# The order of each engine's list, made along a simulated time line instead of from a plain table of durations

## The chip, the cores and the metric

One core of one Trainium2 chip. The time is that of one execution on the device in microseconds, the median of several runs. Five engines have queues of their own, which run in order: TensorE (PE, with its weight loads as PEld), VectorE (DVE), ScalarE (ACT), GpSimd (POOL) and SyncE (SP), which issues the DMAs. They wait for each other by semaphores.

## The reference

Two transformer blocks over 512 rows of width 1024, in float32. The first has a mixer of two halves, 2-D neighbourhood attention with context keys and a Mamba-2 scan (SSD) in both directions, then a gated FFN with a convolution, then a norm. The second has windowed attention with a sink, then a SwiGLU FFN. Modulations come from products of a vector with ada_w.

```python
h = modulate(rms_norm(x, norm1_w), sh1, sc1)
p = h @ w_in
attn = neighbourhood_attention(q, k, v, kc, vc, rpb, rows)
y_ssd, _, _ = ssd_bidirectional(p[..., 3 * NA_WIDTH:col_ssd], xs, bm, cm, dt, a, ssd_d,
                                ssd_norm_w, h_fwd, h_bwd)
x = x + g1 * (jnp.concatenate([attn, y_ssd], axis=-1) @ w_out)
x = x + g2 * conv_glu(modulate(rms_norm(x, norm2_w), sh2, sc2), ffn_w_up, ffn_conv_w, ffn_conv_b, ffn_w_down)
x = rms_norm(x, final_norm_w)
...
x = x + g1 * rmsnorm(windowed_gqa_sink(h, att_w_qkv, att_w_o, att_sink, rel_bias), mix_norm_post)
x = x + g2 * rmsnorm(swiglu(h, ffn_w_in, ffn_w_out), ffn_norm_post)
```

## The kernel before

Every weight comes from memory in float32 as tiles of 128x1024 (`wr`, three buffers, DMA on SP in `fetch`, L132). `load_w` splits a tile in a high part (`wh`, ACT, L152) and a low part (`wl`, DVE, L153), and each product is three matmuls (`mm3`, L89 to L91; `step` in `nat_out`, L829). In between, `load_w` lets one step of the vector products with ada_w run (`gemv`: an `ada` tile by DMA, L226, and one operation on DVE, L230).

The stages in order, with the time at which they run: the prologue, where x and the rows of `ada` (L182) make the modulated features h for eight feature blocks of 128 (`gemv2`, L322; `columns`, L330; `features`, L342), to 70 us; the tiles of the projection, beginning with those for the scan (x_bc); the SSD (`ssd`, L590 to L640: L593 and L617 sums and products, L605 spreads, L629 and L634 outputs, on DVE and POOL between them) beside the first `project`s (rope on ACT, DVE, POOL, L681 to L684), about 112 to 197 us; neighbourhood attention (`attend`, L743 to L775) and the last projections, to 345; w_out and the first norm, to 397; the FFN; the norm into the second block at 755; the projections of the second attention from 777 and its heads from 811 to 919; w_o; the second FFN from 970.

A norm is turned to features by `turn` (L913, called by `tick` after a set count of products), and the features are split on DVE (L920, L921). In the second attention each head has four score tiles: PE L1053 and L1054 into a bank of scores (three of them), DVE L1056 adds the bias, ACT L1058 takes exp, PE L1069 transposes into one of two banks, ACT L1073 and DVE L1074 split, PE L1080 multiplies with v into one bank; ACT L1086 and DVE L1087 add its halves, and per pair of heads L1097 and L1098 divide. Products of the next projection (L89 to L91) are free to stand between these rows.

```python
        hi, lo = WH(F32R, 1024), WL(F32R, 1024)
        act(hi[:, :n], raw[:, :n], AF.Copy)
        V.tensor_sub(lo[:, :n], raw[:, :n], hi[:, :n])
        step_jobs()
...
                tr(pt[:, 128 * i:128 * i + 128], sc[:, 128 * i:128 * i + 128], ident)
...
            act(hi, src, AF.Copy)
            V.tensor_sub(lo, src, hi)
```

The order in which an engine gets its instructions is not that of the code. A scheduler takes every instruction as soon as what it needs is done by its reckoning, and writes one list for each engine. By default it reckons with a table of durations; nothing in the kernel sets an order by hand but the counts of `tick`.

## Time and profile before

| | |
|---|---|
| median of 3 runs | 1336.83 us (1335.62 to 1337.73) |
| the profiled execution | 1336.04 us, span 1334.2 |
| busy of the span | PE 97%, DVE 61%, ACT 45%, POOL 7% |
| DMA | 168.12 MB, mean 126 GB/s |

Busy time counts what an engine does; the rest of the span it waits. A PE that is 97% busy leaves little to be had. The windows cut the span by time: each row has a stretch, its length, and the busy time of PE, PEld, DVE, ACT and POOL in it with the number of instructions, then the clock granted to PE (1.00 is 2.4 GHz), the share of time in which the DMA engines were busy, and the rate. The chain of waits follows what ended last back to what released it.

### The profile page before, as it was taken

The page shows a single profiled execution, that of the slowest core. Times are in us where ns is not written, and L with a number is a line of the kernel's source. Part 1 is how long each engine was busy: PE and PEld are TensorE (multiplying, and loading weights), DVE is VectorE, ACT ScalarE, POOL GpSimd, SP SyncE. Part 2 cuts the span into 40 slices and gives each one's busy share as a digit, 9 for nine tenths or more (in the row PEclk, how much of TensorE's full clock was granted, in tenths as well). Part 3 has the DMA queues.
Part 4 walks back from the last instruction along what each step waited for, and adds up shares of the span by engine and source line. Part 5 has one row for each costly group of instructions (what it writes and reads, how often), then busy time and mean ns, then how long its engine had stood idle before and what let it go on. Part 6 is the DMA issues. An engine that isn't in the chain of part 4 may idle for free.

```text
span 1334.2 us, 17792 instructions
## 1 busy us (share of the span) xinstructions
PE 1296.5 (97%) x6751; PEld 1082.7 (81%) x6751; DVE 813.3 (61%) x1491; ACT 599.1 (45%) x1090; POOL 94.9 (7%) x101
## 2 busy tenths in 40 slices
PE   8999999999999999999999999999999999999997
PEld 4687778998879888888788788878798888888886
DVE  5887996566685766675953667997644232334333
ACT  3546546675454333333433557886652222233321
POOL 0013550000000000000000310000100000000000
PEclk9999999999999999999999999999999999999999
DMA  8763131133553654664754213112133333332221
GB/s 306 261 190 114 45 103 56 43 124 112 207 196 103 221 171 160 221 207 171 239 172 142 69 39 97 47 47 93 56 111 95 95 95 95 97 102 101 95 79 64
DMA packets 53237, 168.12 MB, mean 126 GB/s; under 512 B 6048, under 2 KB 11424, under 8 KB 53152
## 3 DMA queue, kind: packets, MB, share of 16 engines
q1 hardware_dynamic: 53152, 166.99, 38.5%
q8 instruction: 53, 0.87, 0.3%
q14 instruction: 32, 0.26, 0.1%
HBM read 164.87 MB, written 2.10 MB: 125 GB/s over the span
## 4 chain that ended last, share of the span: by engine, by line
PE 77%; DVE 10%; DMA 5%; ACT 4%; issue 2%; POOL 2%; SPq 0%; POOLq 0%; DVEq 0%; ACTq 0%
PE bank L829 18%; PE bank L90 16%; PE bank L89 16%; PE bank L91 16%; PE bank L769 2%; PE bank L1080 1%; DVE wl L153 1%; DMA ada<-in_ada_w 1%; PE bank L1069 1%; DMA wr<-in_w_in 1%; PE bank L763 1%; DVE acc L230 1%; POOL sm L211 1%; ACT wh L152 1%; DVE hl L921 1%
## 5 line engine op out<-in xcount | busy, mean ns | idle before, releaser
L90 PE MATMUL bank<-hl,wh 128*128 128x512 f32 (+1 forms) x1040 | 387.2, 372 | 2.1 <-DVE hl L921 1.5
L91 PE MATMUL bank<-hh,wl 128*128 128x512 f32 (+1 forms) x1040 | 387.7, 373 | 0.0
L89 PE MATMUL bank<-hh,wh 128*128 128x512 f32 (+1 forms) x1040 | 386.0, 373 | 0.1
L152 ACT ACTIVATE wh<-wr 128x1024 fp32r<-128x1024 f32 x173 | 182.2, 1058 | 386.3 <-PE bank L90 270.3
L153 DVE TENSOR_TENSOR wl<-wr,wh 128x1024 fp32r<-128x1024 f32 x173 | 212.9, 1232 | 196.6 <-ACT wh L152 196.2
L90 PEld LDWEIGHTS bank<-hl,wh 128*128 128x128 f32 x1040 | 196.4, 189 | 34.3 <-DVE hl L921 2.1
L89 PEld LDWEIGHTS bank<-hh,wh 128*128 128x128 f32 x1040 | 196.0, 189 | 34.0 <-DVE hh L920 0.8
L91 PEld LDWEIGHTS bank<-hh,wl 128*128 128x128 f32 x1040 | 196.5, 189 | 31.0
L829 PE MATMUL bank<-wh,act 128*128 128x512 f32 x544 | 146.2, 389 | 0.0
L829 PEld LDWEIGHTS bank<-wh,act 128*128 128x128 f32 x544 | 102.1, 188 | 21.5 <-issue 0.3
L230 DVE SCALAR_TENSOR_TENSOR acc<-ada,cs,acc 128x1024 f32<-128x1024 f32 x70 | 89.9, 1284 | 19.9 <-DMA ada<-in_ada_w 19.6
L976 DVE TENSOR_TENSOR act<-bank,act 128x512 f32<-128x512 f32 x44 | 30.4, 690 | 92.9 <-PE bank L91 92.7
L829 PE MATMUL bank<-wl,act 128*128 128x512 f32 x272 | 84.1, 389 | 0.0
L211 POOL TENSOR_TENSOR sm<-sm,mh 128x1 f32<-128x1 f32 x28 | 17.3, 618 | 648.3 <-DVE sm L210 648.3
L829 PEld LDWEIGHTS bank<-wl,act 128*128 128x128 f32 x272 | 51.0, 188 | 10.6
L829 PE MATMUL bank<-act,act 128*128 128x512 f32 x240 | 56.7, 397 | 0.0
L829 PEld LDWEIGHTS bank<-act,act 128*128 128x128 f32 x240 | 46.0, 192 | 9.6
L986 DVE TENSOR_TENSOR act<-act,act 128x512 fp32r<-128x512 f32 x44 | 29.5, 687 | 21.9 <-PE bank L829 21.9
L971 ACT ACTIVATE act<-act 128x512 f32<-128x512 f32 x22 | 13.9, 633 | 57.4 <-DVE act L970 57.4
L916 ACT ACTIVATE tm<-bank,mod 128x128 f32<-128x128 f32 x96 | 35.8, 458 | 7.2 <-PE bank L913 4.2
L985 ACT ACTIVATE act<-act 128x512 fp32r<-128x512 f32 x44 | 26.7, 623 | 24.1 <-DVE act L986 21.5
L895 POOL TENSOR_TENSOR xn<-x,ada 128x512 f32<-128x512 f32 x8 | 10.5, 1313 | 354.8 <-DVE x L869 350.8
(335 smaller groups left out, 1989.7 us busy)
## 6 DMA issues: line engine op xcount, KB each, us to landing
ada<-in_ada_w SPq DMA_DIRECT2D x80, 512.0 KB, 4.3
wr<-in_ffn_w_up_tiles SPq DMA_DIRECT2D x44, 512.0 KB, 4.5
wr<-in_ffn_w_in_tiles SPq DMA_DIRECT2D x44, 512.0 KB, 3.6
wr<-in_ffn_w_down SPq DMA_DIRECT2D x22, 512.0 KB, 4.4
wr<-in_ffn_w_out SPq DMA_DIRECT2D x22, 512.0 KB, 3.3
wr<-in_w_in_tiles SPq DMA_DIRECT2D x19, 512.0 KB, 4.2
wr<-in_att_w_qkv_tiles SPq DMA_DIRECT2D x10, 512.0 KB, 3.7
ada<-in_ada SPq DMA_DIRECT2D x8, 512.0 KB, 5.6
```

Of the source, the lines that this page charges most:

```text
L89: mm(o, lh, rh, start=start, stop=False)
L90: mm(o, lh, rl, start=False, stop=False)
L91: mm(o, ll, rh, start=False, stop=stop)
L152: act(hi[:, :n], raw[:, :n], AF.Copy)
L153: V.tensor_sub(lo[:, :n], raw[:, :n], hi[:, :n])
L211: GP.tensor_tensor(ms[:, 1:2], ms[:, 0:1], mhalf, op=ALU.pow)
L230: V.scalar_tensor_tensor(acc, raw, csil[:, ci + k:ci + k + 1], acc, op0=ALU.mult, op1=ALU.add)
L829: mm(ps[tb][a], l, r[a], start=start and l is lh and r is w[0], stop=stop and l is ll)
L916: act(full[:, 128 * i:128 * i + 128], p[:, 128 * i:128 * i + 128], AF.Identity, scale=mod[:, 8 + k:9 + k], bias=mod[:, k:k + 1])
L976: V.tensor_mul(actT[ft], p, actT[ft])
L985: act(hi, actT[k], AF.Copy)
L986: V.tensor_sub(lo, actT[k], hi)
```

## The change

One argument. The scheduler that makes the lists now keeps a time line on which it plays the queues, and orders by it.

```diff
-    with tile.TileContext(nc) as tc:
+    with tile.TileContext(nc, schedule_with_timeline_sim=True) as tc:
         tile_hybrid_then_windowed_gqa(tc, aps, out)
```

The instructions are the same ones; only ACT_TABLE_LOAD, which stands wherever ACT changes its table of functions, goes from 11 to 15. The lists move, as at these two places.

SP's list in the prologue, where the loads for the features are issued: `ada` and `n` are the two kinds of rows of the modulation for a feature block, `wr` a weight tile. Before:

```order
L132 DMA wr_207<-in_w_in 128x1024
L182 DMA ada_201<-in_ada 128x1024
L182 DMA ada_247<-in_ada 128x1024
L182 DMA n_249<-in_ada 128x512
L182 DMA n_251<-in_ada 128x512
L182 DMA n_297<-in_ada 128x512
L182 DMA n_299<-in_ada 128x512
L182 DMA ada_295<-in_ada 128x1024
L132 DMA wr_301<-in_w_in 128x1024
```

After, the same place, where the list goes on with a constant:

```order
L132 DMA wr_207<-in_w_in 128x1024
L182 DMA n_249<-in_ada 128x512
L182 DMA n_251<-in_ada 128x512
L182 DMA n_297<-in_ada 128x512
L132 DMA wr_301<-in_w_in 128x1024
L411 DMA tri<-in_consts 128x512
L411 DMA cosT<-in_consts 128x512
L411 DMA sinT<-in_consts 128x512
L182 DMA ada_201<-in_ada 128x1024
```

And further down in the new list:

```order
L132 DMA wr_511<-in_w_in_tiles 128x1024
L132 DMA wr_513<-in_w_in_tiles 128x1024
L182 DMA ada_295<-in_ada 128x1024
L182 DMA n_393<-in_ada 128x512
L376 DMA n_426<-in_ctx 128x512
L182 DMA ada_341<-in_ada 128x1024
L376 DMA n_427<-in_ctx 128x512
L376 DMA n_428<-in_ctx 128x512
L132 DMA wr_733<-in_w_in_tiles 128x1024
L132 DMA wr_773<-in_w_in_tiles 128x1024
L182 DMA ada_389<-in_ada 128x1024
L376 DMA n_429<-in_ctx 128x512
```

Three constants now stand ahead of `ada_201`, and four tiles of the later projection (`wr_511`, `wr_513`, `wr_733`, `wr_773`) ahead of `ada_389` and `ada_459`, the rows of the last two feature blocks. Before, all `ada` rows up to `ada_459` came first.

PE's list in the second attention, from where the projection's products for the bank `bank_7664` begin; L1053 and L1054 are scores, L1069 transposes, L1080 products with v. Before:

```order
L89 MATMUL bank_7664<-hh_6466,wh_7660 128x512
L90 MATMUL bank_7664<-hl_6467,wh_7660 128x512
L1069 MATMUL bank_7441<-id_107,xn_7417 128x128 x3
L1080 MATMUL bank_7452<-p_7428,v_7097 128x256
L1053 MATMUL bank_7536<-q_6930,q_7327 128x256
L1054 MATMUL bank_7536<-q_6933,q_7327 128x256
L91 MATMUL bank_7664<-hh_6466,wl_7661 128x512
L1069 MATMUL bank_7447<-id_107,xn_7423 128x128 x2
L1080 MATMUL bank_7452<-p_7429,v_7097 128x256
L89 MATMUL bank_7664<-hh_6466,wh_7660 128x512
L1080 MATMUL bank_7452<-p_7428,v_7097 128x384
L1053 MATMUL bank_7583<-q_6930,q_7330 128x256
```

After, from the nineteenth product of the same bank; the eighteen ahead of it follow one another without another row between:

```order
L89 MATMUL bank_7664<-hh_6466,wh_7660 128x512
L90 MATMUL bank_7664<-hl_6467,wh_7660 128x512
L1053 MATMUL bank_7583<-q_6930,q_7330 128x256
L1054 MATMUL bank_7583<-q_6933,q_7330 128x256
L1053 MATMUL bank_7589<-q_6930,q_7330 128x384
L1054 MATMUL bank_7589<-q_6933,q_7330 128x384
L1069 MATMUL bank_7441<-id_107,xn_7417 128x128 x3
L1053 MATMUL bank_7595<-q_6930,q_7330 128x384
L1080 MATMUL bank_7452<-p_7428,v_7097 128x256
L1054 MATMUL bank_7595<-q_6933,q_7330 128x384
L1069 MATMUL bank_7447<-id_107,xn_7423 128x128 x2
L1080 MATMUL bank_7452<-p_7429,v_7097 128x256
```

Before, one to three products stand between the attention's rows; after, the first twenty of this bank follow one another, and the attention's rows behind them stand together.

## Rows read from the trace of the kernel before

**Rows 1.** Busy time and instructions of each engine, from the page.
```profile
PE 1296.5 (97%) x6751; PEld 1082.7 (81%) x6751; DVE 813.3 (61%) x1491; ACT 599.1 (45%) x1090; POOL 94.9 (7%) x101
```

**Rows 2.** The chain that ended last, by engine, from the page.
```profile
PE 77%; DVE 10%; DMA 5%; ACT 4%; issue 2%; POOL 2%; SPq 0%; POOLq 0%; DVEq 0%; ACTq 0%
```

**Rows 3.** Windows by stage: length, busy us per engine (instructions), clock, DMA share, GB/s.
```profile
0.00:70.00 70.00, 64.84 (x364) 39.87 (x365) 47.20 (x128) 29.11 (x47) 3.30 (x9) 0.98 0.79 273
...
112.00:197.00 85.00, 76.86 (x417) 61.22 (x416) 74.75 (x114) 42.55 (x75) 51.13 (x47) 1.00 0.26 78
...
197.00:300.00 103.00, 101.17 (x700) 92.08 (x700) 65.89 (x184) 68.89 (x132) 6.43 (x5) 1.00 0.22 72
...
300.00:311.00 11.00, 8.83 (x43) 7.33 (x42) 9.46 (x12) 4.51 (x6) 0.00 (x0) 0.84 0.80 239
...
755.00:777.00 22.00, 17.35 (x81) 14.59 (x80) 18.49 (x37) 14.21 (x39) 9.73 (x10) 0.88 0.07 19
...
811.00:894.00 83.00, 82.53 (x484) 69.44 (x483) 75.82 (x213) 69.45 (x192) 0.00 (x0) 1.00 0.20 61
...
894.00:919.00 25.00, 21.73 (x122) 18.44 (x121) 22.72 (x64) 20.05 (x57) 0.00 (x0) 0.93 0.10 27
...
945.00:970.00 25.00, 23.44 (x132) 19.45 (x131) 18.31 (x39) 20.06 (x52) 4.86 (x7) 1.00 0.09 22
...
970.00:1322.00 352.00, 352.00 (x1629) 294.63 (x1628) 121.53 (x142) 101.19 (x140) 1.78 (x3) 1.00 0.30 93
...
1322.00:1334.00 12.00, 5.08 (x23) 3.87 (x21) 4.59 (x9) 1.37 (x4) 1.10 (x2) 0.89 0.24 88
```

**Rows 4.** Timeline of PE in the prologue: start, duration, instruction, count.
```profile
41.48 0.40 PE L90 MATMUL bank<-hl,wh 128*128 128x512 f32 x1
41.72 0.39 PE L91 MATMUL bank<-hh,wl 128*128 128x512 f32 x1
...
48.05 0.64 PE L322 MATMUL bank<-ada,sel 128*32 128x256 f32 x8
...
64.59 0.40 PE L89 MATMUL bank<-hh,wh 128*128 128x512 f32 x1
```

**Rows 5.** Windows of the prologue, columns as in the windows by stage.
```profile
2.00:40.00 38.00, 35.39 (x197) 19.40 (x195) 21.43 (x59) 11.31 (x20) 1.91 (x2) 0.96 0.95 331
40.00:50.00 10.00, 9.54 (x66) 6.33 (x66) 7.35 (x23) 4.04 (x8) 0.69 (x1) 1.00 0.94 321
```

**Rows 6.** Chain from 112 to 197 us: start, length, what.
```profile
121.75 2.15 POOL r L684
...
145.45 1.26 DVE a L638
...
165.10 1.13 DVE wl L153
```

**Rows 7.** Timeline of ACT around a table load.
```profile
313.11 1.28 ACT L760 ACT_TABLE_LOAD   x1
314.41 0.72 ACT L760 ACTIVATE sc<-sc,ss 128x512 f32<-128x512 f32 x1
```

**Rows 8.** Chain from 755 to 777 us.
```profile
765.69 1.67 DVE hl L921
...
770.45 2.12 DVE x L925
...
775.02 1.97 PE bank L913 x8
```

**Rows 9.** What PE waited for: total us, times, longest.
```profile
PE bank L913 <- DVE xn L906: 6.0, 5, 2.7
```

**Rows 10.** DVE's groups by form from 811 to 894 us.
```profile
L1074 DVE TENSOR_TENSOR p<-bank,p 128x384 fp32r<-128x384 f32 x24 | 13.2, 553 | 2.3 <-ACT p L1073 2.1
...
L1074 DVE TENSOR_TENSOR p<-bank,p 128x256 fp32r<-128x256 f32 x24 | 10.0, 416 | 0.7 <-ACT p L1073 0.5
...
L1056 DVE CUSTOM_DVE_ANT_0 xn<-bank,bi,nsink 128x384 f32<-128x384 f32 x14 | 8.3, 610 | 0.1
...
L1056 DVE CUSTOM_DVE_ANT_0 xn<-bank,bi,nsink 128x256 f32<-128x256 f32 x14 | 6.7, 477 | 0.1
...
L1087 DVE TENSOR_TENSOR tm<-bank,tm 64x512 f32<-64x512 f32 x11 | 7.5, 686 | 1.8 <-ACT tm L1086 1.8
```

## The prediction

> **What bounds the kernel now.** I read the busy table first: TensorE (PE) is busy 1296.5 of 1334.2 us, DVE 813.3, ACT 599.1 [rows 1]. So whatever an order can give back is small: 37.7 us in which PE shows no work. The chain that ended last says the same, 77% PE, but also 10% DVE and 5% DMA [rows 2]. Then I cut the span into its stages [rows 3]; the reader is to see where PE's time is below the stretch's length. The second FFN gives nothing away: 352.00 of 352.00 us. The idle time stands in the prologue (5.16 in 70 us), the SSD stretch 112 to 197 (8.14), a stall at 300 to 311 (2.17), the turn into the second block at 755 to 777 (4.65), the end of the second attention at 894 to 919 and the norm behind it (3.27 and 1.56), and the last write-out (6.92). These are lower figures: a 128x512 matmul is recorded with some 390 ns, yet they start 0.23 us apart [rows 4], so the last one before a gap covers some 0.16 us of it. I take the stages' idle time as what can be won, and know that it may be half as much again.
>
> **What the change moves.** No work comes or goes, but for four table loads on ACT. The two orders of PE are the same over most of both FFNs. They differ in the prologue, between about 100 and 412 us, from 755 to 797 and from 812 to 969. So there are six terms.
>
> *Prologue.* SP's queue now puts seven loads that are needed late ahead of the feature blocks' modulation rows: three constants of 256 KB and four weight tiles of 512 KB, 2.9 MB in all. By counting the list, 13.8 MB have to land before the eighth feature block before the change, 16.7 MB after it. DMA is 94 to 95% busy from 2 to 50 us, so order counts there. By the rates, 12.6 MB are in at 40 us and 13.8 MB at 44 us; the eighth block's gemv (L322) starts at 48.05 [rows 4, 5]. It had some 4 us in hand. 2.9 MB at the 321 GB/s of that stretch are 9 us, so the block starts 5 us late, and some of that is filled, since weights that came early let other products run. Bounds: 0, if the blocks find enough other work, to +9, if they find none and had nothing in hand. I take **+4**.
>
> The Trainium skill, "DMA: Bandwidth & Descriptors", section "Queues, rings and completion order", says that on each DMA engine descriptors are consumed in ring order, so a load that is put ahead on SP's queue is paid by those behind it. The busy shares above agree with it, and it speaks against this change.
>
> *SSD stretch.* Here the chain of waits leaves PE for tens of us: 115 to 130 us and 136 to 175 us are ACT, DVE and POOL [rows 6]. DVE is busy 74.75 of 85 us, POOL 51.13, so the stretch is nearly DVE's. What the order can do is start DVE's work earlier and put PE's filling products where DVE is behind. I added up, along both orders, DVE's work that a PE row needs less PE's work up to it: the largest lead that DVE needs is 12.1 us before and 5.9 us after. So up to 6 us of the 8.14 can go. Against it stands one stretch of PE's new list with 10.95 us of chain work and no filling product, which DVE feeds with some 17 us. Bounds: +5 (that stretch stalls for 17 less 11.0, and nothing else is won) to -8 (all idle time). I take **-5**.
>
> *197 to 397 us.* PE idles 1.83 us to 300 and 2.17 in the stall behind it [rows 3]. Filling products are spread finer in the neighbourhood attention, but four table loads join ACT there or soon after, as sigmoid- and exp-like lines (L656 and L760) now alternate. A load takes 1.28 us, and the next ACTIVATE starts 0.02 us behind its end [rows 7]. Four are 5.1 us; ACT is busy 68.89 of 103 us in that stretch, so most is covered, and where an exp waits for it one load shows. Bounds: -4 (all of it goes) to +5 (all loads show). I take **+1**. The Trainium skill, "ScalarE: Activation LUTs", section "What ACT_TABLE_LOAD costs", gives 2.66 us for each switch, drain included; that would be 10.6 us for the four. The trace differs: 1.3 us from the load's start to the next function's.
>
> *755 to 777 us.* The chain is the norm on DVE from 757 to 775, and PE waits for L906's xn [rows 8, 9]. The new order turns the third and the fourth row block about 4 and 2.5 us of PE's work later, with products of three banks between. So 2.5 to 4 of 4.65 go: bounds 0 to -4.65, I take **-3**.
>
> *Second attention, 811 to 894 us.* Today it runs almost without idle time: PE 82.53 of 83.00, while DVE has 75.82 and ACT 69.45 [rows 3]. It does so since products (L89 to L91) stand between the heads' rows in pieces of 0.2 to 1.1 us. The new list has them in blocks of 2 to 4.5 us, and between them chains of 4.6 to 9.8 us without one. Of its 75.82 us for 48 score tiles DVE can do only a part without PE: L1056 on a bank of scores (0.48 to 0.61 us, three banks), L1074 on a bank of transposes (0.42 to 0.55 us, two banks), and perhaps two operations of 0.69 on an output [rows 10]. That is 2.6 to 4.0 us of work in hand. What a block is longer than that, DVE stands: for the blocks of 4.07, 3.16, twice 4.52 and twice 3.39 us it adds up to 1.1 us with 4.0 in hand, and to 7.4 with 2.6. DVE's own idle time, 7.2 us of 83, may take it all in; ACT, which stands between L1056 and the transposes and is 84% busy, may run dry as well, half as much again. So the bounds are 0 and +11; I take the middle of 1.1 and 7.4, **+4**.
>
> *894 to 970 us.* The w_o products of four banks are now put between the last heads in pieces of 2.71 us, where 3.27 and 1.56 us were idle. Bounds: -4.8 to +3 (one of them holds up the last head). I take **-3**.
>
> The sum is 4 - 5 + 1 - 3 + 4 - 3 = **-2 us**. The profiled run took 1336.04 us (span 1334.2 and 1.8 around it), 0.8 below the median of 1336.83. So 1334 us.
>
> **Rivals.** *A, gains and losses about cancel* (the sum): 1334, own range 1327 to 1341. *B, only the gains come:* attention's blocks are covered, early weights fill the prologue. -5 - 3 - 3 and 0 for the rest is -11, so 1325. For it: DVE has 7.2 us to spare in the 83 of the second attention. Against it: the bytes in the queue are plain. *C, the other side: the second attention becomes DVE's.* Its place is 811 to 894; from the point where a block of products is longer than DVE's work in hand (2.6 to 4.0 us), each us of it is one that DVE lacks in the chain behind it, and it has but 8.6% of idle time to give. +11 in place of +4 and a prologue at +5 make 1342; with no gain in the SSD stretch (+5) and all of the loads (+4) 1351. For it: DVE's and ACT's busy shares, 91% and 84% [rows 3]. Against it: four of the six blocks are hardly longer than the work in hand. *D, the order does not decide:* queues are in order, but waits end on the same late operations, and the span stays within 1 us: 1336.
>
> **How the numbers follow.** A measurement of this kernel tells about 0.2% (2.7 us) from nothing. Chances: A 0.40, B 0.23, C 0.27, D 0.10. A lies half below 1334.2 (0.19), 0.14 within 0.2% and 0.07 above; B is faster; C is slower; D is the same (0.09), but for 0.01 on the slow side. Together: faster 0.42, same 0.23, slower 0.35. The time is A's, **1334 us**. The range reaches to B's and C's middle and beyond: 1318 (B with all 8 us of the SSD stretch and the stall at 300) to 1352 (C in full).
>
> **What would show it.** In the windows after: prologue, PE's first product of the x_bc tiles some 4 us later than 64.59 [rows 4], DMA share no lower; SSD stretch shorter by 5 us with the same DVE time; at 755 a PE busy share near 95% in place of 79%; in the second attention PE waits of the kind L1069 or L1080 for DVE or ACT, where 82.53 of 83 is busy now, and 3 to 5 us more from its first score to its last. Wrong would be: SSD stretch no shorter (then DVE's total was the bound, not its start), the prologue not later (then other work fills it), or an attention that is as full as before.

## The result and the profile after

The changed kernel took 1410.73 us (median, 1409.58 to 1416.82), the kernel before 1337.28: a ratio of 1.0556 (95% interval 1.0532 to 1.0579), 73 us slower. The forecast was 1334, with 1318 to 1352 as its range. It was wrong in sign and far off in size.

The busy table of the changed kernel, from its page:

```profile
PE 1316.9 (94%) x6751; PEld 1102.0 (78%) x6751; DVE 823.2 (58%) x1491; ACT 606.1 (43%) x1094; POOL 94.4 (7%) x101
```

Beside [rows 1] PE is busy 20.4 us longer on the same 6751 matmuls, and its idle time in the span of 1407.8 us is 90.9 where it was 37.7: 53.2 more. The two make up the whole difference of the spans, 73.6 us. So the reader has two things to look for: where PE waits, and why the same work takes it longer.

Windows of both kernels, cut where the same instructions end (the dt products' transposes L441, the last SSD output L629, the last product of the first FFN, the second attention's first score L1053, its last L1080). The columns are those of [rows 3]. Before:

```profile
0.00:69.00 69.00, 63.84 (x358) 38.99 (x359) 46.73 (x126) 28.92 (x46) 3.30 (x9) 0.98 0.79 275
69.00:197.00 128.00, 119.86 (x686) 100.18 (x687) 110.33 (x173) 66.22 (x109) 57.43 (x51) 1.00 0.39 117
197.00:770.00 573.00, 563.77 (x2906) 478.46 (x2906) 373.17 (x664) 259.50 (x433) 21.93 (x24) 0.99 0.46 153
770.00:811.00 41.00, 38.33 (x307) 38.09 (x306) 26.19 (x44) 22.66 (x44) 4.48 (x6) 0.96 0.16 52
811.00:923.00 112.00, 108.25 (x627) 91.20 (x626) 101.41 (x282) 90.33 (x252) 0.00 (x0) 0.98 0.20 60
923.00:1334.00 411.00, 402.51 (x1877) 335.74 (x1874) 155.51 (x204) 131.49 (x209) 7.75 (x12) 1.00 0.29 92
```

After:

```profile
0.00:86.00 86.00, 71.55 (x383) 44.82 (x383) 59.89 (x137) 31.85 (x49) 3.75 (x9) 0.94 0.81 280
86.00:234.00 148.00, 131.68 (x746) 113.12 (x746) 111.65 (x178) 72.47 (x122) 55.20 (x52) 0.97 0.25 74
234.00:803.00 569.00, 551.58 (x2822) 468.04 (x2821) 364.75 (x644) 253.21 (x416) 24.04 (x24) 0.99 0.46 151
803.00:844.00 41.00, 37.54 (x305) 36.50 (x305) 27.14 (x48) 24.20 (x48) 4.54 (x6) 1.00 0.19 60
844.00:997.00 153.00, 127.05 (x657) 107.01 (x656) 103.97 (x282) 93.37 (x252) 0.00 (x0) 0.91 0.15 46
997.00:1407.00 410.00, 397.51 (x1847) 332.47 (x1845) 155.76 (x204) 130.99 (x209) 6.85 (x12) 0.99 0.29 91
```

Row by row, the length grows by 17, 20, -4, 0, 41 and 0 us (the last row ends 1 us before the span does). PE's idle time (length less busy) grows by 9.3 in the prologue, 8.2 in the SSD stretch, 8.2 from there to the end of the FFN, 0.8, 22.2 in the second attention, and 4.0 behind it. The lengths count work that changed places too: PE issues 746 matmuls in the second row in place of 686, and 84 fewer in the third. The second attention is the plainest case, 153 us in place of 112. It has 657 matmuls in place of 627; 26 of the 30 more are products of w_o (L829) that ran behind the last output before. At the 0.23 us by which such products start apart they are some 6 us (an estimate), so some 35 of the 41 us are loss. The last row has 30 matmuls fewer and is no shorter.

There PE waits for what it hardly waited for before. What PE waited for in the second attention, total, times and longest, after:

```profile
PE bank L1069 <- DVE p L1074: 14.9, 12, 2.7
PE bank L1080 <- ACT p L1073: 5.0, 6, 0.9
PE bank L1080 <- DVE p L1074: 3.4, 3, 1.4
```

and before:

```profile
PE bank L1069 <- DVE p L1074: 1.3, 2, 0.7
...
PE bank L1080 <- ACT p L1073: 0.2, 1, 0.2
```

One round of it, PE's timeline of the changed kernel (start, duration, instruction, idle time before it and who ended it):

```profile
907.43 0.62 PE L1080 MATMUL bank<-p,v 128*128 128x384 f32 x2 [1.45 <-DVE p L1074]
907.89 0.60 PE L1097 MATMUL bank<-id,rx 128*128 128x128 f32 x4
908.25 0.65 PE L1080 MATMUL bank<-p,v 128*128 128x384 f32 x3
908.74 0.38 PE L1069 MATMUL bank<-id,xn 128*128 128x128 f32 x2
910.98 1.05 PE L1069 MATMUL bank<-id,xt 128*128 128x128 f32 x6 [1.86 <-DVE p L1074]
912.97 0.39 PE L1080 MATMUL bank<-p,v 128*128 128x256 f32 x1 [0.94 <-ACT p L1073]
```

and what ACT and DVE do in it:

```profile
911.53 0.49 ACT L1073 ACTIVATE p<-bank 128x384 fp32r<-128x384 f32 x1 [0.93 <-PE bank L1069]
...
912.44 0.48 ACT L1073 ACTIVATE p<-bank 128x384 fp32r<-128x384 f32 x1
```

```profile
909.16 0.48 DVE L1056 CUSTOM_DVE_ANT_0 xn<-bank,bi,nsink 128x256 f32<-128x256 f32 x1 [1.45 <-PE bank L1069]
909.68 0.69 DVE L1087 TENSOR_TENSOR tm<-bank,tm 64x512 f32<-64x512 f32 x1
910.41 0.43 DVE L1074 TENSOR_TENSOR p<-bank,p 128x256 fp32r<-128x256 f32 x1
910.75 0.68 DVE L1098 TENSOR_TENSOR tm<-tm,bank 128x512 f32<-128x512 f32 x1
...
912.18 0.55 DVE L1074 TENSOR_TENSOR p<-bank,p 128x384 fp32r<-128x384 f32 x1
```

From 907.43 to 914 PE's list has nothing but the attention's rows. The transposes of 910.98 wait 1.86 us until DVE's L1074 has emptied a bank; L1073 on ACT waits 0.93 us for these transposes; L1080 on PE waits 0.94 us for L1073. Each engine waits for the last one's turn, and no product stands between to be done meanwhile. DVE is busy 104 of the stage's 153 us, so it isn't its total that binds.

The second thing is the clock. It is granted at 0.91 over this stretch, where it was 0.98, and in places far less:

```profile
860.00:880.00 20.00, 15.92 (x72) 13.33 (x71) 16.48 (x47) 12.98 (x37) 0.00 (x0) 0.74 0.24 74
425.00:437.00 12.00, 9.01 (x45) 8.27 (x46) 9.64 (x21) 11.00 (x31) 0.55 (x1) 0.57 0.17 45
```

A mean of 0.91 between the two levels, 1.2 and 2.4 GHz, means that 18% of 153 us, some 27 us, ran at the lower one. Half of it at most, 14 us, is lost to that, out of the 18.8 us by which PE's busy time in the stage grew; the products of w_o that moved in are some 6 of these 18.8. Over the whole run the mean granted clock is 0.974 in place of 0.993: some 73 us at the lower level in place of some 19, so at most 27 us more are lost to it, and PE's busy time grew by 20.4. The same can be seen in single rows: two scores of 256 columns that started 0.12 us apart in the kernel before start 0.21 us apart at 915.20 and 915.41 after. The Trainium skill, "TensorE: Matmul & The Clock Gate", section "HAM oscillation — how this bites in real kernels", tells of a kernel whose PE falls to the lower clock at each wait for DMA and does its next work slowly; the trace agrees in kind, with 0.74 and 0.57 in these two stretches, but the waits in them are for DVE and ACT.

In the SSD stretch the waits are few and long. PE's timeline there, after:

```profile
205.91 1.11 PE L593 MATMUL bank<-t,n 128*128 128x256 f32 x4 [4.06 <-DVE n L597]
...
217.97 0.46 PE L617 MATMUL bank<-b,b 128*128 128x128 f32 x2 [1.20 <-DVE sc L618]
...
222.84 0.71 PE L605 MATMUL bank<-a,sel 128*128 128x512 f32 x2 [2.18 <-DVE t L636]
...
226.10 0.56 PE L753 MATMUL bank<-b,b 128*128 128x256 f32 x1
```

This is the stretch that the prediction named, PE's list without a filling product. It holds 10.95 us of work by the prediction's count, and it takes 27 us:

```profile
199.40:226.10 26.70, 17.82 (x85) 13.43 (x83) 25.25 (x37) 10.45 (x19) 13.95 (x14) 0.90 0.29 88
```

DVE is busy 25.25 of these 26.7 us, so it sets the pace here, and not with the chain alone. Ahead of two rows that PE waits for stands other work in DVE's new list:

```profile
202.88 2.28 DVE L153 TENSOR_TENSOR wl<-wr,wh 128x1024 fp32r<-128x1024 f32 x1
205.09 0.68 DVE L597 TENSOR_TENSOR n<-bank,n 128x512 f32<-128x512 f32 x1
...
219.26 2.72 DVE L700 TENSOR_TENSOR b<-r,b 64x512 fp32r<-64x512 f32 x2
222.00 0.69 DVE L636 TENSOR_TENSOR t<-bank,ex 128x512 f32<-128x512 f32 x1
```

L153 splits a weight tile and L700 the keys of the neighbourhood attention; the SSD rows behind them end PE's waits of 4.06 and 2.18 us. All of DVE's other work in the stretch (L153, L275, L682, L683, L700, L714) is 9.0 us, and what is left, some 16, is close to the 17 that the prediction had for the chain. PE idles 8.9 us here, of 16.3 in the stage. The longest single wait, 4.8 us at 159.18, is ahead of this stretch: there DVE's L582 stands behind a vector product (L230) that itself waits 2.0 us for its `ada` tile.

### The profile page after: what moved, and what is told of

It reads as the page before. It is cut to its first block, busy times and chain, and to the rows that moved or that the text cites. A ratio compares the mean times of both kernels' runs of the same rounds, so it can differ in the third digit from the quotient of the medians.

```text
span 1407.8 us, 17816 instructions
## 1 busy us (share of the span) xinstructions
PE 1316.9 (94%) x6751; PEld 1102.0 (78%) x6751; DVE 823.2 (58%) x1491; ACT 606.1 (43%) x1094; POOL 94.4 (7%) x101
## 4 chain that ended last, share of the span: by engine, by line
PE 62%; DVE 5%; ACT 1%; issue 1%; DMA 0%; POOL 0%; DVEq 0%; POOLq 0%; ACTq 0%
PE bank L829 20%; PE bank L89 12%; PE bank L90 12%; PE bank L91 12%; PE bank L1080 1%; PE bank L1069 1%; DVE wl L153 1%; PE bank L1053 1%; PE bank L1054 1%; DVE p L1074 1%; PE bank L913 0%; DVE acc L230 0%; DVE tm L1087 0%; DMA ada<-in_ada_w 0%; ACT wh L152 0%
## 5 line engine op out<-in xcount | busy, mean ns | idle before, releaser
L153 DVE TENSOR_TENSOR wl<-wr,wh 128x1024 fp32r<-128x1024 f32 x173 | 212.4, 1233 | 198.3 <-ACT wh L152 195.9
L829 PE MATMUL bank<-wh,act 128*128 128x512 f32 x544 | 146.2, 389 | 0.2 <-ACT wh L152 0.2
L829 PEld LDWEIGHTS bank<-wh,act 128*128 128x128 f32 x544 | 102.0, 188 | 21.8 <-ACT wh L152 0.7
L230 DVE SCALAR_TENSOR_TENSOR acc<-ada,cs,acc 128x1024 f32<-128x1024 f32 x70 | 91.4, 1305 | 33.4 <-DMA ada<-in_ada_w 32.9
L829 PE MATMUL bank<-wl,act 128*128 128x512 f32 x272 | 84.2, 389 | 0.1
L829 PEld LDWEIGHTS bank<-wl,act 128*128 128x128 f32 x272 | 51.0, 188 | 11.1 <-DVE wl L153 0.5
L829 PE MATMUL bank<-act,act 128*128 128x512 f32 x240 | 55.5, 390 | 0.0
L829 PEld LDWEIGHTS bank<-act,act 128*128 128x128 f32 x240 | 44.9, 188 | 9.2
L1080 PE MATMUL bank<-p,v 128*128 128x256 f32 (+1 forms) x128 | 37.4, 383 | 9.0 <-ACT p L1073 5.0
L916 ACT ACTIVATE tm<-bank,mod 128x128 f32<-128x128 f32 x96 | 35.4, 476 | 13.0 <-PE bank L913 12.5
L985 ACT ACTIVATE act<-act 128x512 fp32r<-128x512 f32 x44 | 26.7, 624 | 30.4 <-DVE act L986 29.0
L1074 DVE TENSOR_TENSOR p<-bank,p 128x256 fp32r<-128x256 f32 (+1 forms) x64 | 30.4, 485 | 14.2 <-ACT p L1073 12.8
```

Of the source, the lines that this page charges most:

```text
L230: V.scalar_tensor_tensor(acc, raw, csil[:, ci + k:ci + k + 1], acc, op0=ALU.mult, op1=ALU.add)
L829: mm(ps[tb][a], l, r[a], start=start and l is lh and r is w[0], stop=stop and l is ll)
L916: act(full[:, 128 * i:128 * i + 128], p[:, 128 * i:128 * i + 128], AF.Identity, scale=mod[:, 8 + k:9 + k], bias=mod[:, k:k + 1])
L1080: mm(po[:, 128 * n0:128 * n1], vv[j][:, 128 * kvh:128 * kvh + 128], part[:, a:a + 128 * (n1 - n0)], start=j == 0 and part is ph, stop=j == ...
```

## The experiments

An engine's list can be fixed from within the kernel: an edge without a semaphore from each instruction to the next of the same engine, in a given order, and the scheduler then builds the other lists around it. So parts of one kernel's order can be set into the other. What is computed stays the same in all of them. Ratios are against the kernel before, run beside each (medians from 1335 to 1339 us).

Only what is set is fixed. Where one engine's list is set, the scheduler also moves rows of the others, and the run shows that list together with the lists that were made around it. The order of starts in the traces tells how far. Of DVE's 281 instructions in the second attention the changed kernel has 167 in the order of the kernel before; e1 has 167 too, e2 183, e11 201, e12 191. In e5 and e10 the lists of the stages that were put back are those of the kernel before, but for a few rows of ACT and POOL in e10. The edit, the same for all but for the lists:

```diff
+def keep_order(tc, nc):
+    no_sync = mybir.DependencyInfo(mybir.DependencyClass.NoSync, mybir.DependencyReason.DATA)
+    known = {i.name: i for i in nc.cur_bb.bb.instructions}
+    for lists in ORDER.values():
+        for text in lists:
+            names = [f"I-{n}" for n in text.split()]
+            for first, then in zip(names, names[1:]):
+                tc.add_manual_dep(known[then], first, no_sync, reason="order")
...
         tile_hybrid_then_windowed_gqa(tc, aps, out)
+        keep_order(tc, nc)
```

Theory 1: PE's list of the second attention, with its products in blocks, costs the 41 us by itself. The rival: DVE's and ACT's new lists do.

**e1, before with PE's new list of the second attention.**

```diff
+ORDER = {
+    "PE": [
+        "7488 7489 7490 7491 7492 7493 7494 7495 7496 7497 7498 7499 7500 7501 7502 7503 7504 7505 7175 7176 "
...
```

> The kernel before, with only PE's list of the second attention and w_o (835 instructions) put in the order of the changed kernel; the scheduler with the table of durations fits the other lists around it. Theory 1, PE's blocks of products cost the stage its 41 us by themselves: about 1337 + 41 = 1378 us (1368 to 1388). Rival, DVE's and ACT's new lists cost it: within 10 us of 1337.

1381.48 us, ratio 1.0314 (1.0291 to 1.0337): 42 us slower, the size that theory 1 has. The stage from the first score to the last output, windows of this run:

```profile
815.80:969.20 153.40, 128.65 (x654) 109.12 (x653) 104.94 (x282) 93.20 (x251) 0.00 (x0) 0.89 0.15 46
```

153.4 us with a clock of 0.89, and the wait of L1069 for L1074 stands at 14.8 us, as in the changed kernel (14.9). DVE's list was made anew around PE's, though, and is about as far from the one of before as the changed kernel's is. So this run shows that PE's new list leads to the loss, not that it makes it by itself.

**e2, after with PE's old list there.**

```diff
+ORDER = {
+    "PE": [
+        "7303 7304 7175 7176 7305 7222 7223 7306 7307 7228 7229 7234 7235 7185 7186 7240 7241 7308 7190 7191 "
...
```

> The changed kernel, with only PE's list of the second attention and w_o put back to the order of before. Theory 1: 1411 - 41 = 1370 us (1362 to 1380), and the stage as full as before. Rival (DVE's and ACT's lists): stays above 1400 us.

1391.24 us: 20 us back of 41, between the two theories.

```profile
844.70:976.00 131.30, 111.79 (x624) 89.46 (x623) 102.95 (x282) 93.49 (x251) 0.00 (x0) 0.99 0.17 54
```

The clock is back at 0.99, but 19.5 of 131.3 us are idle. PE's list in the stage is that of the kernel before, row for row, and the stage is still 19 us longer than the 112 there. So the others' lists cost something as well.

**e5 and e6, DVE's and ACT's lists.** Theory 2: the other 20 us are those of DVE's and ACT's lists. In e5 all three are put back; in e6 the kernel before gets DVE's and ACT's new ones and PE's list is left to the scheduler.

```diff
+ORDER = {
+    "PE": [
+        "7303 7304 7175 7176 7305 7222 7223 7306 7307 7228 7229 7234 7235 7185 7186 7240 7241 7308 7190 7191 "
...
+    "DVE": [
+        "6546 7003 6544 6545 6549 6594 6551 6576 6553 6577 6595 6588 6589 6636 6637 6621 6622 6633 6634 6645 "
...
+    "Activation": [
+        "6931 6932 6961 6962 7300 6967 6968 7481 6997 7000 7031 7034 7098 7662 7150 7843 7161 7167 7173 7179 "
...
```

> The changed kernel, with PE's, DVE's and ACT's lists of the second attention and w_o all put back to the order of before (PE's alone gave back 20 us of 41). Theory 2, the other 20 us are those of DVE's and ACT's lists: about 1370 us (1362 to 1378). Rival, they come from elsewhere (the loads' order, what runs ahead of the stage): stays at 1391 us.

1378.39 us, at the edge of theory 2's range. The stage is as it was, in idle time and clock:

```profile
855.40:966.50 111.10, 107.40 (x625) 90.48 (x624) 101.53 (x282) 90.32 (x251) 0.00 (x0) 0.98 0.20 60
```

111.1 us in place of 153 in the changed kernel, all of the 41. PE's list is the same here as in e2, so the 20 us between 131.3 and 111.1 are those of DVE's and ACT's lists. The whole run won only 32 of them: DVE's list was put back from the norm at 755 us on, PE's only from the first score, and the way from the first FFN's end to that score got longer.

```diff
+ORDER = {
+    "DVE": [
+        "6594 6546 6544 6595 7003 6545 6549 6551 6553 6636 6576 6637 6577 6678 6588 6645 6679 6589 6647 6621 "
...
+    "Activation": [
+        "7300 6931 6932 6961 6962 7481 6967 6968 6997 7000 7031 7098 7034 7662 7150 7843 7161 7167 7173 8024 "
...
```

> The kernel before, with only DVE's and ACT's lists from the norm at 755 us to w_o's norm in the new order; PE's list is left to the table's scheduler. Theory 2, these lists cost 15 us or more by themselves: 1352 to 1378 us. Rival, they cost only beside a list of PE that was not made with them: 1331 to 1345 us.

1387.09 us, ratio 1.0370 (1.0327 to 1.0413): some 48 us slower, more than theory 2 had.

```profile
811.00:967.00 156.00, 127.73 (x641) 107.44 (x640) 103.14 (x282) 93.92 (x251) 0.00 (x0) 0.87 0.15 45
```

The list of PE that the scheduler made around these isn't the one of before either. In the stage its products stand in 69 pieces, where the kernel before has 72, of one to nine products, and the changed kernel 21; but up to 68 of the attention's rows follow one another without a product (before 46, changed kernel 73), and four more such stretches have 40 or 41. So this run shows that DVE's and ACT's new lists lead to the whole loss even where PE's products stand in many pieces, not that they make it beside PE's old list. Taken together, e1, e2, e5 and e6 show that the loss is in the lists of the three engines as a set; how much is one list's alone they don't show. That the lists go round with each other, and the slower one sets the pace, is a reading of the waits.

**e11 and e12, blocks in the list of before.** PE's list of before with its own order of the attention's rows, and of each of five banks' 24 products the first twenty drawn together in one block (e11) or two of ten (e12); of the second FFN's first bank as well, where they stand nearly together anyway.

```diff
+ORDER = {
+    "PE": [
+        "7303 7304 7305 7306 7307 7308 7309 7310 7311 7312 7313 7314 7315 7316 7317 7318 7319 7320 7321 7322 "
...
```

> The kernel before, with one thing changed in PE's list of the second attention: of each of five banks' 24 products, the first twenty stand in one block where the first stood; the attention's own rows keep the order of before. Theory 1a, the blocks alone cost it: 1337 + 25 to 45, so 1362 to 1382 us. Rival, the order of the attention's own rows (which head's scores, transposes and outputs stand next to each other) costs it: 1337 to 1345 us.

1363.33 us, ratio 1.0200 (1.0180 to 1.0220): 26 of the 42 us come with the blocks and with DVE's and ACT's lists made around them. PE has the same instructions in the stage as in the kernel before, so none of it is moved work. The other 16 us go with what else e1's list has, the order of the attention's own rows and the products of w_o among them; that wasn't tried apart.

```profile
812.00:949.00 137.00, 120.11 (x629) 100.78 (x628) 102.72 (x282) 92.88 (x252) 0.00 (x0) 0.90 0.17 52
```

```diff
+ORDER = {
+    "PE": [
+        "7303 7304 7305 7306 7307 7308 7309 7310 7311 7312 7175 7176 7222 7223 7228 7229 7234 7235 7185 7186 "
...
```

> As the run with blocks of twenty products, but in two blocks of ten (2.3 us each), the second where the eleventh stood. The prediction priced a block by what it is longer than DVE's work in hand (2.6 to 4.0 us): then blocks of 2.3 us cost nothing, 1335 to 1342 us. Rival: it is the attention's rows left without products between them that cost, and PE waits there for each round through ACT and DVE: more than half of the 25 us stays, 1350 to 1363 us.

1353.55 us, ratio 1.0133 (1.0108 to 1.0158): 18 us stay, in the rival's range.

```profile
811.50:939.20 127.70, 113.87 (x627) 94.47 (x626) 102.84 (x282) 92.20 (x252) 0.00 (x0) 0.96 0.17 55
```

A block of 2.3 us is shorter than any figure that the prediction gave for DVE's work in hand, and still some 3.6 us go with each bank. So the price isn't that of the block's overhang. PE idles 13.8 us here in place of 3.8, in 18 waits of up to 2.1 us for DVE's and ACT's rows of the attention, which fits the rival: the rows that are left without products between them cost it. That it is these rows, and not the lists that were made around the blocks, is argued.

**e4, SP's list of the prologue.**

```diff
+ORDER = {
+    "SP": [
+        "250 252 298 302 648 649 650 202 300 344 652 248 346 392 396 654 659 512 514 296 394 430 342 431 432 "
...
```

> The kernel before, with only SP's list of the prologue (47 loads) in the new order. Theory, the loads put ahead cost the 11 us that the prologue lost: 1348 us (1344 to 1352), all of it lost by 85 us. Rival, PE's new list of the prologue cost it: 1337 to 1341 us.

1342.83 us, ratio 1.0037 (1.0022 to 1.0053): 5 us slower (3 to 7), less than half of what the theory had.

```profile
0.00:74.50 74.50, 63.09 (x356) 38.58 (x356) 49.51 (x128) 28.74 (x46) 2.80 (x9) 0.98 0.77 268
```

To the end of the same rows (L441) it takes 74.5 us, where it was 69, with 11.4 us idle in place of 5.2. These 6.2 us are two thirds of the 9.3 by which PE's idle time in the prologue grew in the changed kernel; the rest is left to the other lists. The loads' order is all that was set, but with it the scheduler moved rows of PE and DVE, too: of PE's rows up to L441 about one in six changed its place. These 5 us agree in direction with the rule cited in the prediction (the Trainium skill, "DMA: Bandwidth & Descriptors", section "Queues, rings and completion order"), that descriptors are consumed in ring order.

**e7, e8 and e10, the stages up to the first FFN.**

```diff
+ORDER = {
+    "PE": [
+        "113 114 115 116 117 118 119 120 168 169 170 171 172 173 174 175 190 191 192 193 210 179 180 211 212 "
...
```

> The changed kernel, with only PE's list up to the first FFN (prologue, SSD, neighbourhood attention, w_out, norm) put back to the order of before. If PE's list costs these stages their 33 us: 1378 us (1370 to 1386). If, as in the second attention, PE's list alone gives back half: 1391 to 1398 us. If the lists of the others and the loads set it: 1405 us or more.

1419.67 us, ratio 1.0613 (1.0564 to 1.0661): nothing is won, and it is rather slower than the changed kernel, whose interval (to 1.0579) overlaps with this one. The old list of PE among the lists that the new scheduler makes around it is no better than the new one.

```diff
+ORDER = {
+    "PE": [
+        "1095 1096 1097 1066 1067 1068 1069 1070 1071 1072 1073 1074 1075 1076 1077 1078 1079 1080 1081 1082 "
...
```

> The kernel before, with only PE's list from the end of the prologue to the first norm (1578 instructions) in the new order. If this list costs the stages behind the prologue their 22 us: 1359 us (1350 to 1366). If the others' lists set it: 1337 to 1343 us.

1377.88 us, ratio 1.0309 (1.0259 to 1.0360): 41 us, more than these stages lost in the changed kernel, and beyond the range expected (1350 to 1366). With the lists that the old scheduler makes around it, PE's new list is worse than with those of its own set.

```diff
+ORDER = {
+    "PE": [
+        "113 114 115 116 117 118 119 120 168 169 170 171 172 173 174 175 190 191 192 193 210 179 180 211 212 "
...
+    "SP": [
+        "202 248 250 252 298 300 296 302 344 342 346 392 394 396 390 430 431 432 433 460 462 464 512 514 648 "
...
```

> The changed kernel, with the lists of all five engines up to the first FFN (prologue, SSD, neighbourhood attention, w_out, norm) put back to the order of before; PE's alone made it slower. If the lists, as a set, cost these stages their 33 us: 1378 us (1372 to 1384), with only the second attention left slow. If something else does: above 1395 us.

1379.55 us, as expected of the set. The windows are those of before again:

```profile
0.00:69.00 69.00, 62.38 (x357) 39.16 (x357) 46.83 (x126) 28.90 (x46) 3.35 (x9) 0.98 0.79 274
69.00:198.00 129.00, 120.80 (x693) 100.90 (x692) 111.07 (x173) 66.61 (x110) 56.54 (x51) 1.00 0.39 117
198.00:768.00 570.00, 560.09 (x2901) 475.15 (x2900) 372.27 (x660) 257.59 (x427) 23.85 (x24) 1.00 0.47 153
```

With e5 this places the loss: 31 us up to the first FFN, by the whole run, and 41 in the second attention, by e5's stage; both are in the lists, taken as sets.

**e3 and e9, the norm at 755 us.** The only term of a gain that the windows after bore out: from the first FFN's down products to the first score, 680.6 to 844.1 us after where it was 644.6 to 810.9, it is 3 us shorter. The turn itself (before, the row from 755.00 in [rows 3]) and the projections behind it, after:

```profile
788.00:810.00 22.00, 21.23 (x123) 18.24 (x122) 19.38 (x40) 13.44 (x37) 11.06 (x11) 1.00 0.06 19
810.00:844.10 34.10, 31.41 (x260) 30.81 (x259) 21.15 (x36) 21.18 (x40) 1.09 (x2) 1.00 0.20 62
```

PE idles 0.8 us at the turn in place of 4.65, and 2.7 behind it, where the kernel before has no idle time (34.00 of 34.00 us from 777 to 811).

```diff
+ORDER = {
+    "PE": [
+        "6590 6591 6592 6596 6597 6598 6599 6600 6601 6602 6603 6604 6605 6606 6607 6608 6568 6569 6570 6571 "
...
```

> The kernel before, with only PE's list of the norm at 755 us (249 instructions) in the new order. The prediction's term, the last turns stand later in PE's work: 3 us faster, 1334 us. Rival, the norm's chain on DVE sets the time wherever the turns stand: 1337 us.

1341.11 us, ratio 1.0027 (1.0012 to 1.0042): slower by 2 to 6 us, which neither the term nor its rival had. From the last down product to the first score:

```profile
768.00:818.00 50.00, 40.03 (x308) 38.82 (x307) 31.93 (x54) 27.32 (x57) 6.54 (x7) 0.90 0.13 43
```

50 us, with 10 of them idle, where it was 41; PE now waits for L920 (hh, DVE) at the first product on the new features, 7.3 us at once, in place of waiting for L906.

```diff
+ORDER = {
+    "PE": [
+        "6590 6591 6592 6596 6597 6598 6599 6600 6601 6602 6603 6604 6605 6606 6607 6608 6568 6569 6570 6571 "
...
+    "DVE": [
+        "6063 5957 6097 9029 6131 9087 6165 5991 6199 9223 6233 6025 6267 9259 9295 6301 6059 9330 6335 6363 "
...
+    "Activation": [
+        "6643 6584 6585 6586 6552 6587 6644 6650 6617 6618 6619 6620 6651 6629 6630 6631 6632 6727 6728 6660 "
...
```

> The kernel before, with PE's, DVE's and ACT's lists of the norm at 755 us in the new order (PE's alone made it slower). If the new lists are better there as a set: 2 to 4 us faster than 1337, and faster than both kernels. If the gain seen in the changed kernel's windows came from products that ran elsewhere: 1337 us or more.

1332.30 us, ratio 0.9963 (0.9949 to 0.9976): 5 us faster than the kernel before (3 to 7), the only version that beats both. Its windows there, from the first down product on:

```profile
644.00:766.00 122.00, 122.00 (x546) 100.66 (x545) 74.18 (x115) 49.55 (x87) 12.90 (x12) 1.00 0.49 159
766.00:807.00 41.00, 37.53 (x306) 36.59 (x306) 27.14 (x48) 24.14 (x48) 4.45 (x5) 1.00 0.16 52
```

and those of the kernel before:

```profile
644.00:770.00 126.00, 124.03 (x547) 102.11 (x547) 75.27 (x118) 51.73 (x91) 10.72 (x11) 0.99 0.47 154
770.00:811.00 41.00, 38.33 (x307) 38.09 (x306) 26.19 (x44) 22.66 (x44) 4.48 (x6) 0.96 0.16 52
```

With DVE's list serving the turns in their new order the down products end 4 us earlier, without idle time in 122 us. Over both rows PE's idle time falls by 1.2 us and its busy time by 2.8, at a clock of 1.00 in place of 0.99 and 0.96.

## Why the prediction was wrong

**What bounds it.** Right that PE was full and that there was little to win. The losing side was sized far too small: even the upper bounds of all six terms add up to 33 us (9 + 5 + 5 + 0 + 11 + 3), so 1369 us, and 73.6 were lost. Idle time grew by 53 us, and 20 more came from busy time, for which no term had a price.

**The prologue, +4.** The step held for the loads: the last row of the gemv (L322) ends at 52.9 us, where it ended at 49.1, and SP's list costs 5 us with the lists made around it (e4). What failed is that the term ends there. The transposes of L441, at 66.5 us before, start at 81.6. Between them PE waits 3.1 us for L387 and 1.9 for L346 on DVE, and from 70 to 86 us the granted clock is 0.79. The prologue's idle time grew by 9.3 us; the rest of its 17 are slower work and 25 matmuls more, which changed their place. The other engines' lists, which changed too, had no term.

**The SSD stretch, -5.** Wrong in sign. The step that failed is the balance of DVE's work against PE's up to each row: it counts the work that a PE row needs, and not the other work that DVE's own new list puts ahead of it. The term against it, 10.95 us of PE's rows without a filling product that DVE feeds with some 17, was on paper with +5 as its price and set aside. There PE waited 4.06, 2.18 and 1.20 us; DVE was busy 25.25 of 26.7 us, 9.0 of them with work that isn't the chain's. The 8.9 us of PE's idle time there alone are more than the +5.

**197 to 397 us, +1.** Too small. From the last SSD output to the end of the first FFN PE's idle time grew by 8.2 us: 2.8 up to w_out, 2.0 in w_out, 5.3 in the first norm, and 1.9 less at the down products (windows cut at 345.2, 393.9, 410.0 and 644.6 us before, at 362.7, 420.8, 439.0 and 680.6 after). The norm had no loss in the term. The kernel before has 0.8 us of idle time there; now PE waits 3.0, 1.2 and 1.2 us for its turns (L913), and the stretch from 425 to 437 us has a clock of 0.57. Two of the table loads show: those of 347.50 and 357.20 us stand directly ahead of the exp (L760) that PE waits for, 2.28 and 1.45 us. What they cost wasn't tried apart.

**755 to 777 us, -3.** The step held at its place: PE is busy 21.23 of 22 us there, 96%, where the prediction looked for a share near 95%. But 2.7 of the 3.9 us come back as idle time in the projections behind, and more than half of the gain over the whole way, in the changed kernel and in e9, is PE's busy time at a better clock, which the term didn't have. So that its size (e9: -5, from -3 to -7) comes near -3 is luck in part. PE's list, which the step gave as the reason, gained nothing when it alone was set (e3).

**The second attention, +4, bounds 0 to +11.** Rival C had its place and its sign, and the sign named for it came, PE's waits at L1069 and L1080 for DVE and ACT. The size was wrong: 41, some 35 of it without the products of w_o that moved in. The step that failed is "What a block is longer than that, DVE stands". It prices the block, from DVE's side, and lets a gap be closed by DVE's 7.2 us of idle time. In e12 blocks shorter than the work in hand keep 18 of the 26 us. What the traces show is rows behind the blocks without products between them, where PE, ACT and DVE wait for each other round by round, on two banks of transposes and one of outputs: PE's idle time in the stage grew by 22.2 us. The second omission is the clock, 1.2 GHz for some 18% of the stage, at most 14 us, which the prediction had seen in [rows 3] (0.84, 0.88, 0.93 where PE idled) and not priced. The third is that the term read PE's list alone: with one and the same list of PE, DVE's and ACT's lists make the stage 131.3 us (e2) or 111.1 (e5).

**894 to 970 us, -3.** No gain: behind the last output PE idles 12.5 us where it idled 8.5. One wait makes 6.1 of it, for L920 in the norm behind w_o, where no wait was over 0.7 us before. The step that failed takes the products put between the last heads for a gain, and doesn't ask what is left to fill the norm behind them; that the moved products are what is missing there wasn't tried.

What stays open: why the simulated time line makes these lists, whether the order of the attention's rows (in the 16 us that e11 doesn't hold) costs by the clock or by waits, and the part of each single list, since the lists around the one that was set changed with it.

## What to carry to other kernels

A list that another scheduler makes is to be judged by what stands between the rows of a chain through several engines: the same products drawn together in blocks made the run 18 to 26 us longer here, even where the blocks were short (e11, e12). Look at each engine's list, not PE's alone, for other work that stands ahead of a row of the chain. Bound the loss by the length of that chain, not by the idle time of before, and add what PE loses when its clock falls; such a bound was not tried as a forecast here. And lists go in sets: with one engine's list set and the others made around it, a stage could be slower than with either full set (e3, e7). So take over all engines of a stage, and only of the stages that got faster (e9).

## What the runs showed that was not expected

PE's clock fell where its waits were short: 0.74 was granted from 860 to 880 us, where its longest wait is 1.9 us, and 0.57 from 425 to 437, where it is 3.0. In e2, with 19.5 us idle in 131.3, it stayed at 0.99; in e6, with 28.3 in 156, it was 0.87. What tells the two apart was not tried.
